# A query projection at the start of a decoder layer: turns of shift moved into the third panel, the fourth panel run unit by unit

## The chip, the cores and the metric

The kernel runs on one core of one Trainium2 chip. Five engines work beside each other, each through its own queue in order: TensorE (PE in the profile; its weight loads are PEld), VectorE (DVE), ScalarE (ACT), GpSimd (POOL) and SyncE (SP), which only issues transfers here. They meet in on-chip memory (SBUF), and TensorE's results are collected in eight banks of PSUM. The metric is the time of one execution on the device in microseconds, the median of several runs. Before the change it was 1857.52 us (three runs, 1857.36 to 1859.39).

## What is computed

One layer of a decoder trunk for 1024 prompt tokens and 8 x 8 sample tokens (1088 in all), width 1024, all in float32. The part that the change touches is the beginning: a modulated RMS norm, and the first of the columns of one input projection.

```
mod = jax.nn.silu(c) @ w_mod + b_mod
shift, scale, gate = jnp.split(mod, 3, axis=-1)
h = rmsnorm(x, norm_g) * (1 + scale[:, None]) + shift[:, None]
proj = h @ w_in
(mg, u, va, za, q, k, vb, ob, zb, ig, fg, p, zc) = jnp.split(proj, split_idx, axis=-1)
```

Behind it come three branches (a spatial gate, an mLSTM with q, k, v, and a causal pooling), their merge, an output projection, the gate and a last RMS norm. All of that is left as it is, but for one operand of the gate.

## The kernel before

**Precision and panels.** Each float32 operand of a matmul is split into a high and a low part: ACT casts the high part, DVE subtracts it from the source for the low part. A product is then three matmuls, high x high, high x low, low x high. Weights come in panels of 1024 x 256; class `Stream` loads them (SP), casts and splits them in quarters of two k each (`whi` by ACT, L132, `wlo` by DVE, L101), and with `defer` set a quarter's subtraction is put off until the next quarter's cast is issued. At most eight quarters are held. A panel times all tokens is six units: two halves f of its columns by three groups g of tokens (`GROUPS`: 364, 362, 362), each unit a PSUM bank, eight k of three matmuls.

**The start.** `start` runs operations by a hand-written string of letters, `PLAN_0 + PLAN_1`. Two query panels (q0, q1) are computed from the raw x, while the norm's factor is not known yet (L614); their rows are multiplied by the factor later, on POOL, and the share of shift is added (`finish_rows`: L705 on POOL, L709 on ACT, L710 on DVE, stores at L711). That share is shift times the panel (letter s, `shift_mm`, L678, copied by ACT at L681) and then turned to columns by four small matmuls on PE and a copy on DVE (letter t, `shift_turn`, L688 and L690). Meanwhile `h_make` (letter m) makes the eight normalised activations h[0..7], high and low (DVE L653, L658, L660, ACT L656, L657), and W prepares a quarter of the third panel's weights. The letter r (`raw_rows`) copies the raw sums of a panel out of PSUM.

**Third and fourth query panel.** `b_panel` computes q2 and q3 from h. `tick` advances generators in the list `side`, `pace / 2` steps at mid-unit and again at the end of a unit; `evac` copies a finished bank to a row on ACT (L859), and the row is stored from POOL's queue (L863). `prep_some` prepares the next panel's quarters at the end of a unit. q2 runs unit by unit, with `finish_rows` of both raw panels and then `gen_factors(0)` and `(1)` beside it. q3 runs with k outermost (`kouter`): all six banks are filled together, and the copies come at the end. Beside it run `gen_factors(2)` and `(3)` and four calls of `put_t4`.

**The factors.** The next 25 panels (`seven`, from L362) take seven products of half-size blocks in place of eight. One set of operands is made of h: `gen_factors(j)` adds high and low of h[j] and h[j+4] (L765), takes four differences (L770 to L773), and splits two of the results (L207 on ACT, L208 on DVE). The fourth difference, `t4`, is split by `put_t4(j)` into the upper tokens of h[j] itself, from the 544th on, so it must come behind every read of these tokens; the original is fetched back from memory (`b12d`) later. The seven panels use other PSUM tiles, `pairs`, over the same banks; the first is `p`. `ORDER` uses `t4` last in each panel.

**Slots.** Activations, factors, rows and many others share 34 SBUF slots of 1088 columns. A slot goes to a new tile when the last instruction that touches the old one, in program order, is done; so it is with PSUM banks. `scs`, the split silu(c), is held from the start to `gen_gate`, which uses it for the gate much later (L897).

Of the kernel before, what the change touches and what calls it, by code (L numbers as in the profile page):

```python
# [8 lines left out]
F32 = mybir.dt.float32  # L9
F32R = mybir.dt.float32r  # L10
AF = mybir.ActivationFunctionType
ALU = mybir.AluOpType
# [7 lines left out]
T = TP + TS  # L20
NH = 4
KT = 8
# [14 lines left out]
class Stream:  # L37
# [111 lines left out]
    def part(self, p, which, k, cols):  # L149

        c = p["cols"]
        o = (k % 2) * c
        return p["u"][k // 2][which][:, o + cols.start : o + cols.stop]
# [5 lines left out]
class Builder:  # L159
# [95 lines left out]
                self.st.step()  # L255


    def b_panel(self, panel, acts, evac, nk=KT, kouter=False, hook=None):

        self.st.need(panel)  # L260
        part = self.st.part
        units = [(f, g) for f in range(2) for g in range(3)]

        def mms(ps, f, g, k):
            g0, n = GROUPS[g]
            ah, al = acts[k]
            fs = slice(f * 128, f * 128 + 128)
            trip = ((0, ah), (0, al), (1, ah))
            for j, (w, a) in enumerate(trip):
                self.PE.matmul(ps[:, :n], part(panel, w, k, fs), a[:, g0 : g0 + n],  # L270
                               start=(k == 0 and j == 0), stop=(k == nk - 1 and j == 2))

        if kouter:
            pss = [self.ps() for _ in units]
            for k in range(nk):
                if hook is not None:
                    hook(k)
                for (f, g), p in zip(units, pss):
                    mms(p, f, g, k)
                self.prep_some(panel, k, nk)  # L280
            self.st.used(panel)
            for (f, g), p in zip(units, pss):
                evac(f, g, p[:, : GROUPS[g][1]])
            return
        for u, (f, g) in enumerate(units):
            p = self.ps()
            for k in range(nk):
                mms(p, f, g, k)
                if k == nk // 2 - 1:
                    self.tick(self.pace / 2)  # L290
            evac(f, g, p[:, : GROUPS[g][1]])
            self.prep_some(panel, u, len(units))
            self.tick(self.pace / 2)
        self.st.used(panel)

    def a_panel(self, panel, acts, stack, evac, cols=256, order=range(9)):
# [169 lines left out]
    def start(self):  # L466
        i, V, A, G, PE, S = self.i, self.V, self.A, self.G, self.PE, self.S
# [5 lines left out]
        def nxt(key):  # L473
            cnt[key] = cnt.get(key, 0) + 1
            return cnt[key] - 1
# [23 lines left out]
        zero = self.zero = self.const([128, 64], "zero")  # L499
# [10 lines left out]
        G.memset(self.mhalf, -0.5)  # L510
        ones = self.const([128, 1], "ones")
        G.memset(ones, 1.0)
        self.scs = self.slot([128, KT, 64], F32R, name="scs")
        V.tensor_copy(self.scs, zero.unsqueeze(1).to_broadcast([128, KT, 64]))
        sc = self.const([128, KT, 9], "sc")
        A.activation(sc, cT, AF.Tanh, scale=0.5)
        V.scalar_tensor_tensor(out=sc, in0=sc, scalar=1.0, in1=cT, op0=ALU.add, op1=ALU.mult)
        V.tensor_scalar(sc, sc, 0.5, None, ALU.mult)
        A.copy(self.scs[:, :, 0:9], sc)
        V.tensor_tensor(out=self.scs[:, :, 32:41], in0=sc, in1=self.scs[:, :, 0:9].bitcast(F32), op=ALU.subtract)  # L520

        am = self.const([128, KT, 9], "am")
        sm = self.const([128, KT, 9], "sm")
# [18 lines left out]
        def mod_mul():  # L542
            n = nxt("mm")
            p = pmod[n] = self.ps()
            w = wsp.pop(n)
            for kk in range(KT):
                for j in range(2):
                    PE.matmul(p[:64, :256], self.scs[:, kk, :], w[kk // 4][j][:, kk % 4, :],
                              start=(kk == 0 and j == 0), stop=(kk == KT - 1 and j == 1))

        def mod_copy():
# [94 lines left out]
        def h_scale(eng):  # L646
            x = xs[nxt("hs")]
            eng.tensor_tensor(out=x, in0=x, in1=rb[0], op=ALU.mult)
# [52 lines left out]
            rows.append(r)  # L701

        def finish_rows(n):
            for f in range(2):
                G.tensor_tensor(out=rows[n][f], in0=rows[n][f], in1=rb[0], op=ALU.mult)  # L705
            yield
            for f in range(2):
                r = rows[n][f]
                A.activation(r[:, :TP], r[:, :TP], AF.Identity, bias=sw[n][:, f, 0:1])  # L709
                V.tensor_tensor(out=bview(r[:, smp]), in0=bview(r[:, smp]), in1=bcol(sw[n][:, f, 1:9]), op=ALU.add)  # L710
                G.dma_start(self.qd[2 * n + f], r)  # L711
                yield
            rows[n] = None
            if n:
                self.scs2 = None
                rb.clear()

        def late_const():
            self.ident = self.cload("ident")

        ops = {
            "1": mod_load, "2": x_load, "3": self.st.load, "4": late_const,
            "w": keep_warm, "S": mod_split, "M": mod_mul, "C": mod_copy, "T": mod_turn,
            "Q": square, "A": lambda: x_scale(True), "V": lambda: x_scale(False), "H": x_high, "L": x_low,
            "W": self.st.step, "P": lambda: mms("high"), "R": lambda: mms("low"),
            "e": rms_sum, "f": rms_rows, "v": lambda: h_scale(V), "g": lambda: h_scale(G), "m": h_make,
            "z": shift_split, "s": shift_mm, "t": shift_turn, "r": raw_rows,
        }
        self.st.ahead = 1
        for what in (self.PLAN_0 + self.PLAN_1).replace(" ", ""):  # L730
# [1 line left out]
        self.st.ahead = 3  # L732
        self.st.used(w1)
        self.st.defer = True
        self.side = [finish_rows(0), finish_rows(1), self.gen_factors(0), self.gen_factors(1)]
        self.B = {n: [None] * 4 for n in range(1, 8)}
        self.t2 = {}
        self.t4 = {}
        self.pace = 2
        self.b_panel(self.pan["q", 2], self.h, self.evac_rows(2, self.qd))  # L740
        self.drain()

        def hook(k):
            for j in range(2):
                if k == j + 1:
                    self.put_t4(j)
            if k in (1, 3):
                self.side = [self.gen_factors(2 + k // 2)]
            self.tick(2)
            if k in (5, 6):  # L750
                self.put_t4(k - 3)

        self.b_panel(self.pan["q", 3], self.h, self.evac_rows(3, self.qd), kouter=True, hook=hook)
        self.drain()
        self.pace = 1

    def gen_factors(self, j):
# [89 lines left out]
            G.tensor_copy(self.hs[:, k, 64:128], hl[:, TP:T].bitcast(F32))  # L847
        self.B = None

    def evac_rows(self, n, dst, scale=None):  # L850

        st = {}

        def evac(f, g, ps):
            g0, w = GROUPS[g]
            if g == 0:
                st[f] = self.slot([128, T], name="row")
            if scale is None:
                self.A.copy(st[f][:, g0 : g0 + w], ps)  # L859
            else:  # L860
                self.A.mul(st[f][:, g0 : g0 + w], ps, scale)
            if g == 2:
                self.G.dma_start(dst[2 * n + f], st.pop(f))  # L863

        return evac

    def gen_gate(self):

        i, V, S, PE = self.i, self.V, self.S, self.PE
        row = self.slot([9, D], name="gate")  # L870
        bm = self.slot([9, D], name="bgate")
        S.dma_start(bm, i["bmodg"].partition_broadcast(9))

        def load(n):
            if n == 4:
                return None
            w = []
            for j in range(2):
                raw = self.slot([128, 4, 256], name="wg")
                S.dma_start(raw, i["w_mod"][8 + n][:, j * 4 : j * 4 + 4, :])  # L880
                w.append([raw, None, None])
            return w

        nxt = load(0)
        yield
        for n in range(4):
            w = nxt
            for j in range(2):
                w[j][1:] = [self.slot([128, 4, 256], F32R, name="wgs") for _ in range(2)]
                self.split(*w[j])  # L890
                yield
            nxt = load(n + 1)
            yield
            p = self.ps()
            for k in range(KT):
                for j in (1, 2):
                    PE.matmul(p[:64, :256], self.scs[:, k, :], w[k // 4][j][:, k % 4, :],  # L897
                              start=(k == 0 and j == 1), stop=(k == KT - 1 and j == 2))
            r = row[:, n * 256 : n * 256 + 256]
            self.A.copy(r, p[32:41, :256])  # L900
            V.tensor_tensor(out=r, in0=r, in1=p[0:9, :256], op=ALU.add)
            V.tensor_tensor(out=r, in0=r, in1=bm[:, n * 256 : n * 256 + 256], op=ALU.add)
            yield
        V.tensor_scalar(row, row, 0.5, None, ALU.mult)
        self.G.dma_start(self.gated, row)
        self.scs = None
        yield


# [936 lines left out]
for _name, _c0, _cnt in _BLOCKS:  # L1846
# [8 lines left out]
    "LPSSRPR1WS3"  # L1855
)
Builder.PLAN_1 = (
    "rW13SeSM1CPP3MS3PCfRTSgMCgPWSvRgTMgCRTvRTPzmWRmsmgPmPWmWgPRRmtms3R3WmW3tr"
)


# [103 lines left out]
```

## Time and profile before

| | |
|---|---|
| median of three runs | 1857.52 us |
| the profiled execution | 1857.86 us, of which its span 1856.1 us |
| mean granted clock of TensorE | 0.985 |
| the third panel's first matmul (L270) | 119.31 us |
| the first matmul of the seven panels (L362) | 176.87 us |

The profile is of one execution, and its times count from the span's start. A row of a timeline gives start, duration, engine, line, operation, what is written and read, the shapes and, in brackets, how long the engine stood idle before it and what ended that. "x6" means six such instructions merged, with the time of all. The list of waits sums such idle times by what ended them. The table by windows gives for each stretch the busy time of PE, PEld, DVE, ACT and POOL with the number of instructions, then TensorE's granted clock (1.00 is full), the share of the transfer engines and GB/s.

### The profile page before, as it was taken

What the parts mean: (1) busy time and instruction counts of PE and PEld (TensorE: products, weight loads), DVE (VectorE), ACT (ScalarE), POOL (GpSimd) and SP (SyncE); (2) the same over time, 40 slices, a digit from 0 to 9 for tenths busy, and PEclk for the clock granted to TensorE, in tenths of its full rate; (3) what the DMA queues carried; (4) which work ended last, traced back from release to release, by engine and by line L of the source; (5) the groups of instructions that cost most, each with busy time, mean ns of one, the idle gap of its engine ahead of it and who ended that gap; (6) DMA issues with size and microseconds to landing.
All of it is one profiled execution on the core that took longest, in us unless ns stands there. A gap on an engine that the chain in (4) does not pass through costs nothing.

```text
span 1856.1 us, 32242 instructions
## 1 busy us (share of the span) xinstructions
PE 1796.1 (97%) x13017; PEld 1777.4 (96%) x13017; DVE 1071.9 (58%) x2003; ACT 586.0 (32%) x1141; POOL 262.3 (14%) x427
## 2 busy tenths in 40 slices
PE   7888999999999999999999999999999999999998
PEld 7888999999999998999999899999999999999998
DVE  7777556665666542434527955664655766564444
ACT  5443333333333332222223125332333231131224
POOL 3440000000000001110011212321101101200023
PEclk8988999999999999999999999999999999999999
DMA  6332323332222334333335754776457577694422
GB/s 252 108 128 74 106 94 94 104 122 80 71 70 76 130 106 150 121 123 101 94 116 189 217 180 125 240 237 201 143 175 231 179 228 208 184 317 142 151 62 97
DMA packets 142152, 270.42 MB, mean 146 GB/s; under 512 B 19377, under 2 KB 66161, under 8 KB 142003
## 3 DMA queue, kind: packets, MB, share of 16 engines
q1 hardware_dynamic: 118786, 184.20, 31.4%
q0 software_dynamic: 23072, 83.91, 13.3%
q8 instruction: 102, 1.67, 0.4%
q14 instruction: 48, 0.39, 0.1%
q10 hardware_dynamic: 144, 0.26, 0.0%
HBM read 179.96 MB, written 88.35 MB: 145 GB/s over the span
## 4 chain that ended last, share of the span: by engine, by line
PE 86%; DVE 8%; issue 2%; DMA 2%; ACT 1%; POOL 1%; SPq 0%; POOLq 0%; DVEq 0%; ACTq 0%
PE ps L270 30%; PE ps L308 15%; PE p L362 8%; PE y L362 8%; PE z L362 8%; PE x L362 4%; PE ps L614 2%; PE ps L316 1%; PE ps L1466 1%; PE ps L1264 1%; PE ps L1485 1%; PE ps L1682 1%; PE ps L1439 1%; PE ps L1468 1%; DMA ss<-in_w_mod_dram 1%
## 5 line engine op out<-in xcount | busy, mean ns | idle before, releaser
L101 DVE TENSOR_TENSOR wlo<-raw,whi 128x512 fp32r<-128x512 f32 (+1 forms) x272 | 189.7, 698 | 115.6 <-ACT whi L132 115.6
L308 PE MATMUL ps<-whi,hhi 128*128 128x256 f32 (+1 forms) x768 | 218.5, 284 | 0.0
L308 PE MATMUL ps<-wlo,hhi 128*128 128x256 f32 (+1 forms) x768 | 216.0, 281 | 0.0
L308 PE MATMUL ps<-whi,hlo 128*128 128x256 f32 (+1 forms) x768 | 215.1, 280 | 0.0
L270 PE MATMUL ps<-hhi,whi 128*128 128x362 f32 (+1 forms) x624 | 208.2, 334 | 5.5 <-DVE C L1494 3.4
L270 PE MATMUL ps<-hlo,whi 128*128 128x362 f32 (+1 forms) x624 | 207.0, 332 | 1.9 <-DMA hlo<-b12d 1.7
L270 PE MATMUL ps<-hhi,wlo 128*128 128x362 f32 (+1 forms) x624 | 206.6, 331 | 0.0
L270 PE MATMUL ps<-yhi,whi 128*128 128x362 f32 (+1 forms) x576 | 190.1, 330 | 3.0 <-DVE mgr L1742 1.6
L270 PE MATMUL ps<-yhi,wlo 128*128 128x362 f32 (+1 forms) x576 | 188.7, 328 | 0.0
L270 PE MATMUL ps<-ylo,whi 128*128 128x362 f32 (+1 forms) x576 | 188.5, 327 | 0.0
L132 ACT CAST whi<-raw 128x512 fp32r<-128x512 f32 (+1 forms) x272 | 162.3, 617 | 44.9 <-DVE raw L123 36.3
L308 PEld LDWEIGHTS ps<-whi,hhi 128*128 128x128 f32 x768 | 144.6, 188 | 0.8 <-issue 0.4
L308 PEld LDWEIGHTS ps<-wlo,hhi 128*128 128x128 f32 x768 | 144.7, 188 | 0.0
L308 PEld LDWEIGHTS ps<-whi,hlo 128*128 128x128 f32 x768 | 144.4, 188 | 0.0
L270 PEld LDWEIGHTS ps<-hhi,whi 128*128 128x128 f32 x624 | 119.2, 191 | 6.7 <-DVE C L1494 3.6
L362 PE MATMUL p<-hhi,whi 128*128 128x272 f32 x400 | 116.1, 290 | 7.3 <-ACT row L859 7.3
L270 PEld LDWEIGHTS ps<-hlo,whi 128*128 128x128 f32 x624 | 119.5, 191 | 2.6 <-DMA hlo<-b12d 2.6
L270 PEld LDWEIGHTS ps<-hhi,wlo 128*128 128x128 f32 x624 | 119.4, 191 | 0.0
L362 PE MATMUL p<-hlo,whi 128*128 128x272 f32 x400 | 116.5, 291 | 0.0
L362 PE MATMUL p<-hhi,wlo 128*128 128x272 f32 x400 | 116.3, 291 | 0.0
L132 ACT CAST whi<-sum 128x512 fp32r<-128x512 f32 x75 | 46.6, 621 | 219.7 <-DVE sum L119 144.0
L270 PEld LDWEIGHTS ps<-yhi,whi 128*128 128x128 f32 x576 | 108.2, 188 | 3.7 <-DVE mgr L1742 1.8
(434 smaller groups left out, 4489.6 us busy)
## 6 DMA issues: line engine op xcount, KB each, us to landing
raw<-in_w_in_dram SPq DMA_DIRECT2D x204, 256.0 KB
mgr<-mgd SPq DMA_DIRECT2D x24, 544.0 KB
raw<-in_w_br_dram SPq DMA_DIRECT2D x48, 256.0 KB
out_dram<-C POOLq DMA_DIRECT2D x36, 256.0 KB, 4.5
ylo<-yd SPq DMA_DIRECT2D x16, 544.0 KB
merd<-mgr POOLq DMA_DIRECT2D x16, 544.0 KB, 6.1
C<-in_state_C_dram SPq DMA_DIRECT2D x32, 256.0 KB
mgd<-mg POOLq DMA_DIRECT2D x14, 544.0 KB, 4.6
```

Of the source, the lines that this page charges most:

```text
L101: self.kb.V.tensor_tensor(out=lo, in0=src, in1=hi.bitcast(F32), op=ALU.subtract)
L132: kb.A.copy(hi, src)
L270: self.PE.matmul(ps[:, :n], part(panel, w, k, fs), a[:, g0 : g0 + n], start=(k == 0 and j == 0), stop=(k == nk - 1 and j == 2))
L308: self.PE.matmul(p[:, :cols], a[:, ts], part(panel, w, k, cs), start=(k == 0 and j == 0), stop=(k == KT - 1 and j == 2))
L316: self.PE.matmul(p[:, :cols], stack[:, k, :], part(panel, j, k, cs), start=(k == 0 and j == 0), stop=(k == KT - 1 and j == 1))
L362: PE.matmul(bank[n][:, g, :HT], w[:, ks], b[:, gs], start=(n in (1, 5, 6, 7) and j == 0 and m == 0), stop=(j == 3 and m == 2), skip_group_ ...
L614: PE.matmul(sums[-1][u][:, :m], self.st.part(w, 1 - ww, k, fs), a[:, g0 : g0 + m], start=(k == 0 and part == "high" and j == 0), stop=(k = ...
L1264: self.PE.matmul(p[:, :n], wsl[:, ww, k, fs], a[:, g0 : g0 + n], start=(k == 0 and j == 0), stop=(k == 1 and j == 2))
L1439: PE.matmul(x["ps"][:, h * 128 : h * 128 + 128], k[:, 2 * h + d, :], q[:, 2 * h + d, :], start=(d == 0), stop=(d == 1))
L1466: PE.matmul(p[:, :258], x["qw"][:, 2 * h + d, :], C[x["hp"]][:, h, d, :], start=(d == 0), stop=False)
L1468: PE.matmul(p[:, :258], x["P"][:, a, h, :], x["vs"][:, b, h, :], start=(x["c"] == 0 and j == 0), stop=(j == 2))
L1485: PE.matmul(p[:, :258], x["ks"][:, a, h, d * 128 : d * 128 + 128], x["vs"][:, b, h, :], start=(j == 0), stop=(j == 2))
```

## The change

`shift_turn` leaves the plan (both letters t are gone) and becomes the first thing of `finish_rows`. All four `gen_factors` are in the side list from the third panel on, with a pace of 2.4 where it was 2; the list isn't drained between the two panels. The fourth panel runs unit by unit too, in the order 2, 1, 0, 5, 4, 3, that is, for each half of the columns the upper tokens first. After its third unit the list is drained; `put_t4` follows after the fifth unit (j = 0, 1) and after the sixth (j = 2, 3). `evac_rows` counts the parts of a row, since they come in another order. `scs` is no longer kept: `gen_gate` makes it again from `sc`.

```diff
-    def b_panel(self, panel, acts, evac, nk=KT, kouter=False, hook=None):
+    def b_panel(self, panel, acts, evac, nk=KT, kouter=False, hook=None, order=(0, 1, 2, 3, 4, 5)):
...
-        units = [(f, g) for f in range(2) for g in range(3)]
+        units = [divmod(u, 3) for u in order]
...
             evac(f, g, p[:, : GROUPS[g][1]])
             self.prep_some(panel, u, len(units))
             self.tick(self.pace / 2)
+            if hook is not None:
+                hook(u)
         self.st.used(panel)
...
         def finish_rows(n):
+            shift_turn()
             for f in range(2):
                 G.tensor_tensor(out=rows[n][f], in0=rows[n][f], in1=rb[0], op=ALU.mult)
             yield
...
-        self.side = [finish_rows(0), finish_rows(1), self.gen_factors(0), self.gen_factors(1)]
+        self.side = [finish_rows(0), finish_rows(1)] + [self.gen_factors(j) for j in range(4)]
...
-        self.pace = 2
+        self.pace = 2.4
         self.b_panel(self.pan["q", 2], self.h, self.evac_rows(2, self.qd))
-        self.drain()
-
-        def hook(k):
-            for j in range(2):
-                if k == j + 1:
-                    self.put_t4(j)
-            if k in (1, 3):
-                self.side = [self.gen_factors(2 + k // 2)]
-            self.tick(2)
-            if k in (5, 6):
-                self.put_t4(k - 3)
-
-        self.b_panel(self.pan["q", 3], self.h, self.evac_rows(3, self.qd), kouter=True, hook=hook)
-        self.drain()
+
+        def hook(u):
+            if u == 2:
+                self.drain()
+            if u > 3:
+                for j in range(2):
+                    self.put_t4(2 * u - 8 + j)
+
+        self.b_panel(self.pan["q", 3], self.h, self.evac_rows(3, self.qd), hook=hook, order=(2, 1, 0, 5, 4, 3))
...
-            if g == 0:
-                st[f] = self.slot([128, T], name="row")
-            if scale is None:
-                self.A.copy(st[f][:, g0 : g0 + w], ps)
-            else:
-                self.A.mul(st[f][:, g0 : g0 + w], ps, scale)
-            if g == 2:
-                self.G.dma_start(dst[2 * n + f], st.pop(f))
+            if f not in st:
+                st[f] = [self.slot([128, T], name="row"), 0]
+            self.A.copy(st[f][0][:, g0 : g0 + w], ps)
+            st[f][1] += 1
+            if st[f][1] == 3:
+                self.G.dma_start(dst[2 * n + f], st.pop(f)[0])
...
+        scs = self.slot([128, KT, 64], F32R, name="scs")
+        V.tensor_copy(scs, self.zero.unsqueeze(1).to_broadcast([128, KT, 64]))
+        self.A.copy(scs[:, :, 0:9], self.sc)
+        V.tensor_tensor(out=scs[:, :, 32:41], in0=self.sc, in1=scs[:, :, 0:9].bitcast(F32), op=ALU.subtract)
...
-    "rW13SeSM1CPP3MS3PCfRTSgMCgPWSvRgTMgCRTvRTPzmWRmsmgPmPWmWgPRRmtms3R3WmW3tr"
+    "rW13SeSM1CPP3MS3PCfRTSgMCgPWSvRgTMgCRTvRTPzmWRmsmgPmPWmWgPRRmms3R3WmW3r"
```

The rest of the diff renames `self.scs` to a local `scs` in `start` and keeps `sc` as `self.sc`.

More of the change, by code (lines that the diff above doesn't have):

```diff
@@ L512, in start @@
         G.memset(ones, 1.0)
-        self.scs = self.slot([128, KT, 64], F32R, name="scs")
-        V.tensor_copy(self.scs, zero.unsqueeze(1).to_broadcast([128, KT, 64]))
-        sc = self.const([128, KT, 9], "sc")
+        scs = self.slot([128, KT, 64], F32R, name="scs")
+        V.tensor_copy(scs, zero.unsqueeze(1).to_broadcast([128, KT, 64]))
+        sc = self.sc = self.const([128, KT, 9], "sc")
         A.activation(sc, cT, AF.Tanh, scale=0.5)
@@ L518, in start @@
         V.tensor_scalar(sc, sc, 0.5, None, ALU.mult)
-        A.copy(self.scs[:, :, 0:9], sc)
-        V.tensor_tensor(out=self.scs[:, :, 32:41], in0=sc, in1=self.scs[:, :, 0:9].bitcast(F32), op=ALU.subtract)
+        A.copy(scs[:, :, 0:9], sc)
+        V.tensor_tensor(out=scs[:, :, 32:41], in0=sc, in1=scs[:, :, 0:9].bitcast(F32), op=ALU.subtract)
         am = self.const([128, KT, 9], "am")
@@ L547, in mod_mul @@
                 for j in range(2):
-                    PE.matmul(p[:64, :256], self.scs[:, kk, :], w[kk // 4][j][:, kk % 4, :],
+                    PE.matmul(p[:64, :256], scs[:, kk, :], w[kk // 4][j][:, kk % 4, :],
                               start=(kk == 0 and j == 0), stop=(kk == KT - 1 and j == 1))
@@ L726, in start @@
             "e": rms_sum, "f": rms_rows, "v": lambda: h_scale(V), "g": lambda: h_scale(G), "m": h_make,
-            "z": shift_split, "s": shift_mm, "t": shift_turn, "r": raw_rows,
+            "z": shift_split, "s": shift_mm, "r": raw_rows,
         }
@@ L848, in seven_panels, with evac_rows @@
         self.B = None
-    def evac_rows(self, n, dst, scale=None):
+    def evac_rows(self, n, dst):
         st = {}
@@ L872, in gen_gate @@
         S.dma_start(bm, i["bmodg"].partition_broadcast(9))
+        scs = self.slot([128, KT, 64], F32R, name="scs")
+        V.tensor_copy(scs, self.zero.unsqueeze(1).to_broadcast([128, KT, 64]))
+        self.A.copy(scs[:, :, 0:9], self.sc)
+        V.tensor_tensor(out=scs[:, :, 32:41], in0=self.sc, in1=scs[:, :, 0:9].bitcast(F32), op=ALU.subtract)
         def load(n):
@@ L896, in gen_gate @@
                 for j in (1, 2):
-                    PE.matmul(p[:64, :256], self.scs[:, k, :], w[k // 4][j][:, k % 4, :],
+                    PE.matmul(p[:64, :256], scs[:, k, :], w[k // 4][j][:, k % 4, :],
                               start=(k == 0 and j == 1), stop=(k == KT - 1 and j == 2))
@@ L905, in gen_gate @@
         self.G.dma_start(self.gated, row)
-        self.scs = None
         yield
```

## The prediction

> **What bounds the kernel now.** I read the page's list of engines and its chain of work first, then the list of waits of TensorE, then the timelines around the two largest.
>
> ```profile
> span 1856.1 us, 32242 instructions
> PE 1796.1 (97%) x13017; PEld 1777.4 (96%) x13017; DVE 1071.9 (58%) x2003; ACT 586.0 (32%) x1141; POOL 262.3 (14%) x427
> ...
> PE ps L688 <- ACT smp L681: 8.0, 1, 8.0
> PE p L362 <- ACT row L859: 7.3, 1, 7.3
> ```
>
> TensorE (PE) is the bound: busy 97% of the span. Time can only be won where it waits or runs at a lower clock. Its two longest waits both lie in the stage that the change rewrites: 8.0 us ahead of the turns of shift (L688), 7.3 us between the fourth query panel and the first seven-panel. They are one event each, so each is worth its full length if nothing takes its place.
>
> The first wait, in the timelines of POOL, DVE, ACT and PE:
>
> ```profile
> 109.13 4.92 POOL L705 TENSOR_TENSOR row<-row,rb 128x1088 f32<-128x1088 f32 x2
> ...
> 106.17 7.97 DVE L653 TENSOR_TENSOR x<-x,sm 128x64 f32<-128x64 f32 x1
> ...
> 114.18 0.24 ACT L657 CAST hhi<-x 128x64 fp32r<-128x64 f32 x1 [10.35 <-DVE x L653]
> ...
> 117.94 0.36 ACT L681 COPY smp<-ps 64x256 f32<-64x256 f32 x1
> ...
> 106.73 0.61 PE L688 MATMUL ps<-c_sel,smp 64*128 64x9 f32 x4
> ...
> 109.18 1.15 PE L614 MATMUL ps<-xlo,whi 128*128 128x364 f32 x6
> 118.36 1.02 PE L688 MATMUL ps<-c_sel,smp 64*128 64x9 f32 x4 [8.03 <-ACT smp L681]
> ```
>
> The reader should follow it backwards. The second turn (118.36) needs a copy that ACT makes at 117.94. That copy stands in ACT's queue behind L657, which waited 10.35 us for a small add on DVE (L653). The add took 7.97 us and ended at 114.14, when POOL's multiplies ended (109.13 + 4.92 = 114.05): DVE is blocked by POOL. So **the copy is late, and with it all that ACT and DVE prepare for the third panel**. The turn is only the first instruction to meet the delay.
>
> The second wait:
>
> ```profile
> 172.93 0.62 ACT L132 CAST whi<-raw 128x512 fp32r<-128x512 f32 x1 [2.26 <-DVE raw L123]
> 173.46 1.19 ACT L207 CAST hhi<-fac 128x544 fp32r<-128x544 f32 x2
> 174.55 2.27 ACT L859 COPY row<-ps 128x364 f32<-128x364 f32 x6
> ...
> 176.87 0.60 PE L362 MATMUL p<-hhi,whi 128*128 128x272 f32 x1 [7.27 <-ACT row L859]
> ```
>
> All six banks of the fourth panel finish together, and their copies (174.55, x6) are queued on ACT behind casts that wait for DVE's factor work. PE starts again when the last copy is done (174.55 + 2.27 = 176.82).
>
> Both waits also cost clock. In the table by windows, the column after POOL is the granted clock:
>
> ```profile
> 35.00:36.00 1.00, 0.65 (x3) 0.65 (x4) 1.00 (x2) 0.00 (x0) 0.00 (x0) 0.85 0.04 16
> 42.00:43.00 1.00, 1.00 (x6) 1.00 (x5) 1.00 (x2) 1.00 (x2) 0.00 (x0) 0.74 0.03 8
> ...
> 114.00:115.00 1.00, 0.00 (x0) 0.00 (x0) 1.00 (x2) 0.82 (x3) 0.05 (x1) 0.60 0.00 0
> ...
> 124.00:125.00 1.00, 1.00 (x6) 1.00 (x6) 0.00 (x0) 0.00 (x0) 0.00 (x0) 0.78 0.01 4
> ...
> 35.35 1.91 PE L614 MATMUL ps<-xlo,whi 128*128 128x364 f32 x6 [3.80 <-DVE xlo L601]
> ```
>
> Full clock is 1.00 and the low one 0.50, so 0.60 over 114 to 115 puts the drop at 114.20, and 0.78 puts the return at 124.44. An idle of 3.80 us ended at 35.35; the drop came at 35.70 and the return at 42.52. The steps between these four times, 6.82, 71.68 and 10.24, are 2, 21 and 3 times 3.41: the clock changes on a beat.
>
> **The change part by part: first wait.** The turns leave the plan and go into the third panel: the first after half of its first unit, the second after its second unit. POOL's multiply of the rows comes after the turn in program order but uses nothing of it, so it still starts at 109.13 and still blocks DVE until 114.1. What PE can do instead is the first unit, limited by the panel's weights, four quarters of two k each, a high half cast by ACT and a low half made by DVE:
>
> ```profile
> 114.33 0.61 ACT L132 CAST whi<-raw 128x512 fp32r<-128x512 f32 x1
> 118.21 0.62 ACT L132 CAST whi<-raw 128x512 fp32r<-128x512 f32 x1
> 120.01 0.62 ACT L132 CAST whi<-raw 128x512 fp32r<-128x512 f32 x1
> ...
> 115.40 0.68 DVE L101 TENSOR_TENSOR wlo<-raw,whi 128x512 fp32r<-128x512 f32 x1
> 121.25 0.68 DVE L101 TENSOR_TENSOR wlo<-raw,whi 128x512 fp32r<-128x512 f32 x1
> ...
> 119.78 0.51 PE L270 MATMUL ps<-hlo,whi 128*128 128x364 f32 x1
> 120.08 0.51 PE L270 MATMUL ps<-hhi,wlo 128*128 128x364 f32 x1
> 125.72 0.33 PE L270 MATMUL ps<-hhi,whi 128*128 128x362 f32 x1
> 129.69 0.33 PE L270 MATMUL ps<-hhi,whi 128*128 128x362 f32 x1
> ```
>
> These are the second to fourth quarters; the first is there before. PE does two k (6 matmuls) by about 110.7, then is idle until the second quarter's cast (114.33 + 0.61 = 114.94), needs its low half at 116.08, does the rest of that quarter and the four small matmuls of the turn, and waits for the third quarter at 118.83. The turn may wait for a bank that ACT's copy empties at 118.30, so I let the second half of the unit start at 119.3. An idle of 4.3 us is longer than the one at 35.35 after which the clock fell, so I take the low clock: a matmul every 0.30 us (120.08 less 119.78). Twelve of them end at 119.3 + 3.6 = 122.9; the last low half (121.25 + 0.68 = 121.93) is in time for the ninth. Today the unit ends at 125.72. With the clock back at 124.44 as now, the second unit has done 5 matmuls by then and needs 19 more at 0.1655 (129.69 less 125.72, by 24): it ends at 127.6. The second turn adds 0.54 (106.73 to the next instruction at 107.27; the 0.61 overlaps it). So the third unit starts at 128.1 instead of 129.69: **1.5 us won, not 8**. The bounds come from the beat: with the clock back one beat earlier the same count gives 2.6, one beat later 0.0.
>
> [...]
>
> **Second wait.** The fourth panel now runs unit by unit, so five of six copies are made while later units run. Copies lag a unit's end as here:
>
> ```profile
> 125.98 0.46 ACT L859 COPY row<-ps 128x364 f32<-128x364 f32 x1 [4.26 <-PE ps L270]
> ...
> 136.21 1.28 DVE L765 TENSOR_TENSOR fac<-hhi,hlo 128x1088 f32<-128x1088 f32 x1
> 172.22 0.68 DVE L123 TENSOR_TENSOR raw<-raw,raw 128x512 f32<-128x512 f32 x1
> 174.13 0.72 DVE L208 TENSOR_TENSOR hlo<-fac,hhi 128x544 fp32r<-128x544 f32 x1 [1.23 <-ACT hhi L207]
> ...
> 169.03 1.65 ACT L207 CAST t<-fac 128x1088 fp32r<-128x1088 f32 x2 [3.83 <-DVE fac L771]
> ...
> 130.42 5.04 POOL L705 TENSOR_TENSOR row<-row,rb 128x1088 f32<-128x1088 f32 x2
> ```
>
> 0.26 after the boundary at 125.72, plus 0.46, plus 0.05 to the waiter, is 0.77: that stays of the 7.27, and 6.5 goes, if ACT is free then. Whether it is free hangs on DVE's factor chain. Today it runs from 136.21 to 172.22, 36.0 us nearly without a gap. In the new order it also holds L123 (0.7) before its end and loses two splits of upper factors (0.72 each, with one wait like the 1.23 shown): 36.0 + 0.7 - 1.4 - 1.2 = 34.1. It starts after POOL's second pair (130.42), which follows from the first unit's copy through ACT's L709 and POOL's queue; that copy comes 2.8 earlier, so the chain starts at about 133.4 and ends at 167.5. ACT's last casts for it end 1.5 before (today at 169.03 + 1.65 = 170.68 against 172.22): 166.0. Behind them ACT makes two copies (2.27 by 6 is 0.38 each) and two casts of upper factors (1.19 the two): free at 168.0. PE ends the sixth unit 1.5 earlier than today (176.87 - 7.27 = 169.6), at 168.1, and its copy wants ACT at 168.4. **The chain just fits, by 0.4 us.** The last two upper splits come behind that copy, and their factor is read last in the next panel.
>
> ```profile
> 182.47 0.42 PE L362 MATMUL y<-t,whi 128*128 128x272 f32 x2
> ...
> 242.83 0.29 PE L362 MATMUL p<-hhi,whi 128*128 128x272 f32 x1
> ...
> 245.85 0.41 PE L362 MATMUL y<-t,whi 128*128 128x272 f32 x2
> ```
>
> With 0.77 us of idle I take the clock to stay up. Its price now: the first 24 matmuls of the next panel take 5.60 us (176.87 to 182.47), later ones 3.02 (242.83 to 245.85): 2.6 won.
>
> **At nothing:** shift's operands for the gate are made again later:
>
> ```profile
> L514 DVE CAST scs<-zero x1: 427/427/427, 0.9 to 0.9; 128x512 fp32r<-128x512 f32 x1
> ```
>
> 0.43 on DVE and two operations on 72 columns instead of 512, once, ahead of PE work that waits for its own weights; without that cover under 1.3 us (three times the row). No DMA is added; the row store only fires when three parts are in, whatever their order. One slot of 34 is freed.
>
> **Sum:** 1.5 + 6.5 + 2.6 = 10.6. The profiled execution took 1857.86 us, 1.76 around its span; 1857.86 - 10.6 = 1847.3. The median shown is 0.34 lower, so I say 1847.0. Everything after 183 is PE work at full clock with few waits, so the gain should stay.
>
> **The rivals.** *The first wait is given back.* The low clock lasts one beat longer, so lead 0.0: gain 9.1, 1848.4. For it: the beat; against it: nothing else. Chance 0.17.
>
> *The factor chain is late.* [...] For it: the copies now stand between the casts in one queue. Chance 0.14.
>
> *A light window drops the clock* though PE idles only 0.77: 2.6 of the sum goes, 1849.6. Chance 0.05.
>
> *Slower: slots.* With all four factors alive (16 activations, 8 + 4 products, 4 sums) 32 of the 34 slots are held besides the rows. If factor tiles get slots whose rows are still being stored, DVE waits for each store, at most 6.0 us:
>
> ```profile
> DMA to landing us min/median/max: 3.0/4.1/6.0
> ```
>
> Three such waits make the chain 18 late, 17.6 after slack: the clock falls again, and 10.6 - 2.6 - 17.6 = -9.6 gives about 1867. It decides from 8.4 us late. Against it: the stores before were long landed. Chance 0.04.
>
> *The change doesn't do what it says:* a wait of PE remains at the panel's end as long as now; only the 1.5 stays, 1855.5. Chance 0.03.
>
> **How the numbers follow.** The forecast has 0.57, its own range 1845.0 to 1849.0 (lead 2.6 to 0.0, copies one microsecond late). With the first rival and the mild half of the second and third, 1844.5 to 1852.0 leaves less than 2 in 10 out. A measurement tells about 0.2% (3.7 us) from no change. Faster by more: all but the slot case, the last rival and the worst of the chain, 0.90; within: 0.06; slower: 0.04.
>
> **What would show it.** L688 no longer among PE's waits; an idle of about 4 us after 110, ended by casts of L132; the panel ending near 168; the wait at L362 under 1 us and the clock 1.00 there; DVE's last factor split near 167.5. A wait at L362 of several us, ended by L859 behind L207, would mean the chain is late; a DMA ending DVE's idle there would mean slots.

## The result, and the profile after

| | before | changed | ratio (95% interval) |
|---|---|---|---|
| first comparison, medians | 1857.47 us (4 runs) | 1847.35 us (4 runs, 1843.83 to 1848.12) | 0.9944 (0.9930 to 0.9957) |
| second comparison, medians | 1858.36 us (15 runs) | 1848.70 us (5 runs, 1845.20 to 1849.63) | 0.9956 (0.9943 to 0.9968) |
| the profiled execution | 1857.86 us, span 1856.1 | 1843.83 us, span 1842.1 | |

The change makes the kernel about 10 us faster, 0.5%. Its profiled execution is the fastest of the first four: it lies 14 us under the profiled one of before, 4 us more than the medians do. The last section comes back to these 4 us.

The list of TensorE's waits in the changed kernel (engine, line and tile, what ended the wait, us in total, times, longest):

```profile
PE ps L270 <- ACT whi L132: 4.4, 1, 4.4
...
PE p L364 <- ACT row L856: 1.3, 1, 1.3
...
PE ps L690 <- ACT smp L683: 0.6, 1, 0.6
```

The wait of 8.0 us at the turns (now L690) is 0.6, and a new wait of 4.4 us stands in its place, ended by a cast of the third panel's weights. The wait ahead of the seven panels (now L364) fell from 7.3 to 1.3. The timelines of DVE, POOL, ACT and PE around the first:

```profile
104.42 8.00 DVE L655 TENSOR_TENSOR x<-x,sm 128x64 f32<-128x64 f32 x1
...
104.89 2.55 POOL L650 TENSOR_TENSOR x<-x,rb 128x1088 f32<-128x1088 f32 x1
107.38 4.94 POOL L708 TENSOR_TENSOR row<-row,rb 128x1088 f32<-128x1088 f32 x2
...
112.60 0.61 ACT L132 CAST whi<-raw 128x512 fp32r<-128x512 f32 x1
...
113.27 0.67 PE L270 MATMUL ps<-hhi,whi 128*128 128x364 f32 x1 [4.36 <-ACT whi L132]
121.45 0.33 PE L270 MATMUL ps<-hhi,whi 128*128 128x362 f32 x1
```

The small add is still blocked for 8.00 us, beside three multiplies of POOL, until POOL is done (107.38 + 4.94 = 112.32); the cast still follows it, and TensorE, which has done two k of its first unit, waits for that cast. The second unit starts at 121.45.

The table by windows (as before: busy times, then the granted clock) shows the low clock in this unit and the full one ahead of the seven panels:

```profile
112.40:121.40 9.00, 7.41 (x22) 6.07 (x23) 8.92 (x19) 7.03 (x14) 0.00 (x0) 0.51 0.22 61
121.40:128.00 6.60, 6.60 (x42) 6.35 (x41) 1.88 (x7) 4.57 (x7) 3.01 (x3) 1.00 0.62 205
165.40:168.00 2.60, 1.33 (x9) 1.03 (x8) 2.60 (x5) 2.60 (x7) 0.46 (x1) 1.00 0.00 0
```

And the end of the fourth panel, in the timelines of DVE, ACT and PE:

```profile
156.42 1.93 DVE L208 TENSOR_TENSOR t<-fac,t 128x1088 fp32r<-128x1088 f32 x2 [1.69 <-ACT t L207]
164.78 1.92 DVE L208 TENSOR_TENSOR t<-fac,t 128x1088 fp32r<-128x1088 f32 x2
...
154.76 0.62 ACT L132 CAST whi<-sum 128x512 fp32r<-128x512 f32 x1 [4.14 <-DVE sum L121]
155.29 1.64 ACT L207 CAST t<-fac 128x1088 fp32r<-128x1088 f32 x2
...
164.98 0.81 ACT L856 COPY row<-ps 128x362 f32<-128x362 f32 x2
165.68 1.20 ACT L207 CAST hhi<-fac 128x544 fp32r<-128x544 f32 x2
166.78 0.47 ACT L856 COPY row<-ps 128x364 f32<-128x364 f32 x1
...
167.30 0.39 PE L364 MATMUL p<-hhi,whi 128*128 128x272 f32 x1 [1.26 <-ACT row L856]
170.43 0.41 PE L364 MATMUL y<-t,whi 128*128 128x272 f32 x2
```

ACT goes without a pause from the factor's casts to two copies, two casts of upper factors and the last copy, which ends at 167.25; TensorE starts then, at full clock: its first 24 matmuls take 3.13 us (167.30 to 170.43), where they took 5.60.

**A common ruler.** Before the stage begins, executions already differ by some us. So stages are compared from the start of the blocked small add (106.17 before, 104.42 after). From the timelines of all profiles, in us after that start:

| profile | the add takes | second unit of the third panel starts | last matmul of the fourth panel starts | wait ahead of the seven panels | their first matmul | first 24 take | stage (last two added) |
|---|---|---|---|---|---|---|---|
| before | 7.97 | 19.55 | 63.10 | 7.27 | 70.70 | 5.60 | 76.30 |
| change, first profile | 8.00 | 17.03 | 61.29 | 1.26 | 62.88 | 3.13 | 66.01 |
| change, second profile | 7.99 | 17.12 | 62.37 | 0.55 | 63.25 | 3.13 | 66.38 |
| new panel only | 7.97 | 19.29 | 62.83 | 1.97 | 65.13 | 4.64 | 69.77 |
| turns only | 7.98 | 17.12 | 61.65 | 7.28 | 69.25 | 4.46 | 73.71 |
| POOL's rows held back | 3.10 | 12.24 | 57.87 | 1.37 | 59.57 | 3.11 | 62.68 |
| plain order | 7.99 | 17.13 | 62.06 | 0.55 | 62.93 | 3.13 | 66.06 |
| wait filled | 8.03 | 17.18 | 62.41 | 0.55 | 63.30 | 3.12 | 66.42 |
| scs kept | 7.99 | 17.04 | 61.30 | 2.50 | 64.13 | 4.64 | 68.77 |
| held back, plain, pace 2.5 | 3.10 | 12.24 | 56.94 | 1.47 | 58.73 | 3.13 | 61.86 |
| the same, pace 2.64 | 3.11 | 13.33 | 59.76 | 0.55 | 60.63 | 3.13 | 63.76 |

The stage of the change is 10.3 and 9.9 us shorter than that of before.

### The profile page after: what moved, and what is told of

Read it like the earlier page. It is cut to its first block, busy times and chain, and to the rows that moved or that the text cites. A ratio compares the mean times of both kernels' runs of the same rounds, so it can differ in the third digit from the quotient of the medians.

```text
span 1842.1 us, 32227 instructions
## 1 busy us (share of the span) xinstructions
PE 1792.3 (97%) x13017; PEld 1773.2 (96%) x13017; DVE 1074.0 (58%) x2005; ACT 585.4 (32%) x1142; POOL 260.6 (14%) x427
## 3 DMA queue, kind: packets, MB, share of 16 engines
q8 instruction: 102, 1.67, 0.4%
## 4 chain that ended last, share of the span: by engine, by line
PE 86%; DVE 7%; issue 3%; ACT 2%; DMA 1%; POOL 1%; SPq 0%; POOLq 0%; DVEq 0%; ACTq 0%
PE ps L270 31%; PE ps L310 15%; PE y L364 8%; PE p L364 8%; PE z L364 8%; PE x L364 4%; PE ps L616 2%; PE ps L318 1%; PE ps L1465 1%; PE ps L1263 1%; PE ps L1484 1%; PE ps L1438 1%; PE ps L1681 1%; PE ps L1467 1%; PE ps L550 1%
## 5 line engine op out<-in xcount | busy, mean ns | idle before, releaser
L364 PE MATMUL p<-hhi,whi 128*128 128x272 f32 x400 | 115.0, 287 | 1.3 <-ACT row L856 1.3
L364 PE MATMUL p<-hlo,whi 128*128 128x272 f32 x400 | 115.3, 288 | 0.0
L364 PE MATMUL p<-hhi,wlo 128*128 128x272 f32 x400 | 115.2, 288 | 0.0
```

The lines of the kernel that those rows point to most:

```text
L364: PE.matmul(bank[n][:, g, :HT], w[:, ks], b[:, gs], start=(n in (1, 5, 6, 7) and j == 0 and m == 0), stop=(j == 3 and m == 2), skip_group_ ...
```

## The experiments

**The change once more**, without an edit.

> The changed kernel once more, beside the other three of this group, so that all four have the same runs of the kernel before. Theory: 10.1 us faster than before (1847.4), with a spread of some 3 us between executions that comes from where the beat of the clock falls after the first wait. Rival, that the first profile of it (1843.8) is the rule and the others are disturbed: 13 to 14 us faster.

Measured: 1848.70 us against 1858.36, 9.7 faster; five executions from 1845.20 to 1849.63. The first profile's 1843.83 was the quickest execution, not the rule.

**The new panel only.**

```diff
         def finish_rows(n):
-            shift_turn()
...
-    "...PRRmms3R3WmW3r"
+    "...PRRmtms3R3WmW3tr"
```

> The turns of shift are back in the plan, all the rest of the change is kept. Theory (the first wait gives only about 1.5 us, because the panel's weights and activations are late anyway): 8 to 9.5 us faster than before, 1 to 2 us slower than the change, and the wait of 8 us at the turns is back. Rival (moving the turns is worth the 4 us by which the wait became shorter, and the clock with it): 5 us faster than before, 5 us slower than the change.

Measured: 1848.13 us, ratio 0.9959 (0.9947 to 0.9971), so 5.4 to 9.8 us faster than before. By time it can't be told from the change. The wait of 8.0 us at the turns is back. In the stage it loses 3.4 to 3.8 us to the change, more than expected, and the ruler says where: the last matmul comes 0.5 to 1.5 later, the wait ahead of the seven panels is 1.97 long, and behind it the low clock returns for one beat (173.4 to 176.8, worked out from the windows), so that the first 24 matmuls take 4.64. The windows of this kernel there:

```profile
172.00:174.00 2.00, 0.94 (x5) 0.95 (x6) 2.00 (x4) 2.00 (x5) 0.53 (x1) 0.85 0.00 0
174.00:176.00 2.00, 2.00 (x11) 2.00 (x10) 1.60 (x3) 0.09 (x1) 0.00 (x0) 0.50 0.89 240
176.00:178.00 2.00, 2.00 (x15) 2.00 (x14) 0.00 (x0) 0.04 (x1) 0.00 (x0) 0.79 0.41 170
```

TensorE is idle from 171 to 173 only, and has half the clock at 174. This execution was also the slowest of its five (1851.67), so the profile shows the bad case. Neither expectation held in full: most of the gain comes from the fourth panel, as the theory says; how much the turns add within the change is between nothing and 3.8 us, and by medians (1848.13 against 1848.70) it is nothing.

**The turns only.** The kernel before, with `shift_turn()` at the head of `finish_rows` and both letters t gone from the plan.

> Only the turns are moved into the third panel, the fourth panel stays with k outermost. Theory: 1 to 2 us faster than before; the wait of about 4.4 us ended by the cast of the panel's second quarter stays, and the second wait of 7.3 us stays. Rival (the parts need each other: without the new fourth panel the lead is lost again in the factor chain of DVE, since the second wait ends with it): 0 to 0.5 us faster.

Measured: 1854.05 us (11 runs), ratio 0.9982 (0.9973 to 0.9991): 1.7 to 5.0 us faster. The waits are as the theory has them:

```profile
PE p L362 <- ACT row L860: 7.3, 1, 7.3
PE ps L270 <- ACT whi L132: 4.3, 1, 4.3
PE ps L688 <- ACT smp L681: 0.6, 1, 0.6
```

The lead at the end of the fourth panel is 63.10 - 61.65 = 1.45 us, and it isn't lost: the seven panels start 1.45 earlier. That decides against the rival. Between medians the gain is 4.3, more than the 1 to 2 expected. In the stage it is 2.6: the lead, and 1.1 less for the first 24 matmuls, because the low clock behind the second wait lasted two beats here (172.8 to 179.7) and three before (172.2 to 182.5). Whether the edit has a part in that isn't shown, and the rest of the 4.3 stays open. The two halves of the change alone, 10.2 and 4.3 between medians, add up to more than the 9.7 of the whole, so the times don't split the gain; the stage has to.

**POOL's rows held back.** The wait behind the first wait, tested by moving POOL's work instead of the waiter:

```diff
         def finish_rows(n):
             shift_turn()
+            if n == 0:
+                late = self.const([128, 1], "late")
+                G.tensor_copy(late, self.pan["q", 2]["u"][3][1][:, 0:1].bitcast(F32))
             for f in range(2):
                 G.tensor_tensor(out=rows[n][f], in0=rows[n][f], in1=rb[0], op=ALU.mult)
```

> The change, with POOL's first multiply of raw rows held back until DVE has made the last low quarter of the third panel's weights (POOL first copies one column of that quarter). Theory (POOL's multiplies block DVE's small add for 8 us, and that is what is behind the wait of 4.4 us): the add takes under 3.5 us, the wait of TensorE at the second quarter shrinks from 4.4 to under 1.5 us, the first unit ends 4 to 5.5 us earlier; but the factor chain can't come as much earlier, so the wait ahead of the seven panels grows by about 2 us: 2 to 5 us faster than the change, 12 to 15 faster than before. Rival (the add waits for its own input, not for POOL): the add still ends where it did, and the kernel is as fast as the change or slower by what POOL's rows come later.

Measured: 1844.98 us, ratio 0.9942 (0.9927 to 0.9956), 8.2 to 13.6 us faster than before. By time it can't be told from the change, whose interval overlaps; in the stage it is 3.3 and 3.7 faster than the change's two profiles. DVE's and POOL's timelines, and the list of TensorE's waits:

```profile
104.94 3.10 DVE L655 TENSOR_TENSOR x<-x,sm 128x64 f32<-128x64 f32 x1
118.43 3.06 DVE L101 TENSOR_TENSOR wlo<-raw,whi 128x512 fp32r<-128x512 f32 x1 [1.27 <-ACT whi L132]
...
105.41 2.54 POOL L650 TENSOR_TENSOR x<-x,rb 128x1088 f32<-128x1088 f32 x1
115.82 0.18 POOL L709 COPY late<-wlo 128x1 f32<-128x1 f32 x1 [7.87 <-DVE wlo L101]
115.96 4.99 POOL L711 TENSOR_TENSOR row<-row,rb 128x1088 f32<-128x1088 f32 x2
...
PE p L364 <- ACT row L859: 1.4, 1, 1.4
PE ps L690 <- ACT smp L683: 1.2, 1, 1.2
```

The add falls from 8 to 3.10 us and now ends with the one multiply of POOL that is left there (105.41 + 2.54 = 107.95); the moved multiplies block another DVE operation at their new place (118.43, 3.06 instead of 0.68). The block is shown: it follows POOL's work. It isn't one instruction that waits for one other: in the change the add outlasts two multiplies that POOL starts at 107.38 or later, 3 us after the add. The add took 8.00 us beside three multiplies, 3.10 beside one; by what means POOL holds DVE up isn't shown here.

The wait at the panel's second quarter is gone, and the first unit ends 4.8 us earlier than in the change (12.24 after 17.03). The seven panels start only 3.3 and 3.7 earlier. DVE's factor chain sets that, as expected: it starts at 129.09 where it was 131.89, which is 3.3 earlier after the add's start, and the last copy stands behind its casts. TensorE itself comes 3.4 and 4.5 earlier to the end of the fourth panel; against the first profile it had already lost 1.4 in the second unit, in a low clock that lasted until 15.3 after the add's start. So the wait grew by 0.1 and 0.8, less than the 2 us named.

**Plain order of units**, all splits of upper factors at the end:

```diff
         def hook(u):
             if u == 2:
                 self.drain()
-            if u > 3:
-                for j in range(2):
-                    self.put_t4(2 * u - 8 + j)
+            if u == 5:
+                for j in range(4):
+                    self.put_t4(j)
 
-        self.b_panel(self.pan["q", 3], self.h, self.evac_rows(3, self.qd), hook=hook, order=(2, 1, 0, 5, 4, 3))
+        self.b_panel(self.pan["q", 3], self.h, self.evac_rows(3, self.qd), hook=hook)
```

> The change with the fourth panel in its plain order of units (0 to 5), and all four splits of upper factors after the sixth unit. Theory (what counts is that copies are made unit by unit; the upper tokens first buy nothing, since the split factor is read some 18 us into the next panel, and two of its casts stand ahead of the last copy in ACT's queue): the wait ahead of the seven panels is 0 to 1.2 us shorter than in the change, the time within 1.5 us of it, 9 to 12 us faster than before. Rival (the order is what makes room: four splits in a row after the panel hold up ACT and DVE for the seven panels): a new wait of TensorE of 2 us or more within the first seven-panel, 2 to 4 us slower than the change.

Measured: 1845.86 us, ratio 0.9934 (0.9920 to 0.9948), 9.7 to 14.9 faster than before. The stage, 66.06, is the change's own; no new wait of 2 us. ACT's last copy waits 0.91 us for TensorE, where in the change it stood behind two casts. Upper tokens first bring nothing that these times or the stage show.

**The wait filled.** TensorE works in the wait of 4.4 us; the forty products are never read.

```diff
                 mms(p, f, g, k)
+                if warm and u == 0 and k == 1:
+                    for _ in range(warm):
+                        self.PE.matmul(p[:, 368:512], part(panel, 0, 0, slice(0, 128)), acts[0][0][:, 0:144],
+                                       start=True, stop=True, skip_group_check=True)
```

> The change, and in the wait of 4.4 us TensorE does 40 matmuls of 144 columns into unused columns of the first unit's bank; their results are never read. Theory (the wait costs its length and then the low clock, which lasts whole beats of 3.41 us at 1.7 us each): the granted clock stays 1.00 from 107 to 122, the first unit ends about 1 us earlier, limited by the panel's last quarter, and the second is at full speed at once: 1 to 2.5 us faster than the change, 10.5 to 13 faster than before. Rival (the low clock lies under other waits and costs nothing more): as fast as the change, or slower by what the filling runs over (under 1 us).

Measured: 1850.48 us, ratio 0.9962 (0.9950 to 0.9975), 4.6 to 9.3 faster than before. The theory failed here. By time the run can't be told from the change, whose intervals overlap. PE's timeline:

```profile
108.77 4.59 PE L291 MATMUL ps<-hhi,whi 128*128 128x144 f32 x40
116.54 0.75 PE L694 MATMUL ps<-c_sel,smp 64*128 64x9 f32 x4 [1.21 <-ACT smp L687]
```

and the table by windows, two of one beat each:

```profile
113.43:116.84 3.41, 1.67 (x9) 1.06 (x9) 3.41 (x8) 2.99 (x6) 0.00 (x0) 1.00 0.21 77
116.84:120.25 3.41, 3.35 (x12) 2.65 (x11) 3.33 (x8) 3.06 (x7) 0.00 (x0) 0.50 0.27 77
```

The filling held the clock through the wait, and then it fell all the same, at 116.84, after a beat in which TensorE was busy for 1.67 of 3.41 us and never idle longer than 1.21. The second unit started at 17.18, as without it. The stage, 66.42, is that of the change's second profile (66.38).

**The slot of scs kept.** `scs` stays in `self` and `gen_gate` uses it, as before the change.

```diff
-        scs = self.slot([128, KT, 64], F32R, name="scs")
+        scs = self.scs = self.slot([128, KT, 64], F32R, name="scs")
...
-        scs = self.slot([128, KT, 64], F32R, name="scs")
-        V.tensor_copy(scs, self.zero.unsqueeze(1).to_broadcast([128, KT, 64]))
-        self.A.copy(scs[:, :, 0:9], self.sc)
-        V.tensor_tensor(out=scs[:, :, 32:41], in0=self.sc, in1=scs[:, :, 0:9].bitcast(F32), op=ALU.subtract)
+        scs = self.scs
```

> The change with the split silu(c) kept in its slot from the start to the gate, as before, so that one slot less is free. Theory (slots are not what holds the factor chain): within 1 us of the change apart from the beat of the clock, and no idle time of DVE or ACT in the two panels that a transfer ends. Rival (the freed slot is what lets all four factors be alive at once): DVE or ACT waits 3 to 6 us for a store of a query row, and the wait ahead of the seven panels grows to 3 us or more, 3 to 6 us slower than the change.

Measured: 1847.49 us (4 runs), ratio 0.9951 (0.9938 to 0.9965), the change's time. No transfer ends a wait of DVE or ACT in the two panels, but a slot does, in ACT's list of waits between 160 and 170 and in the timelines of DVE and ACT:

```profile
ACT whi L132 <- DVE raw L123: 4.7, 1, 4.7
ACT row L856 <- DVE t L208: 1.1, 1, 1.1
...
165.54 1.92 DVE L208 TENSOR_TENSOR t<-fac,t 128x1088 fp32r<-128x1088 f32 x2
166.91 0.82 ACT L856 COPY row<-ps 128x362 f32<-128x362 f32 x2 [1.08 <-DVE t L208]
```

The copy of the fourth unit needs a new row, and its slot is that of the last factor, which DVE is still reading. That 1.1 us puts the wait ahead of the seven panels at 2.50, and a beat of low clock followed it (4.64 for the first 24 matmuls). So the freed slot is worth 1.1 us at that copy; with the beat the stage of this profile is 2.4 and 2.8 longer than the change's two. The time can't resolve it.

**All of it, with a pace of 2.5:** POOL's rows held back, plain order, `self.pace = 2.5`.

> POOL's first rows held back as in the run before, the plain order of units with all splits of upper factors after the sixth, and a pace of 2.5, so that the third factor's split comes ahead of the stream's sum, which cost DVE an idle of 1.69 us. Theory (after POOL's block is gone the factor chain of DVE and ACT's queue set the end of the panel; each of the three edits shortens it): the wait ahead of the seven panels under 0.8 us, the seven panels start 3.5 to 5 us earlier after POOL's block than in the change: 13 to 16 us faster than before. Rival (what is left ahead of the seven panels is the plain delay of the last copy, and the pace changes nothing): as fast as the run that only holds the rows back, 12 to 13.5 us.

Measured: 1842.95 us, ratio 0.9925 (0.9913 to 0.9938), 11.5 to 16.2 faster than before; the stage is 4.1 to 4.5 shorter than the change's. The wait ahead of the seven panels was 1.47, not under 0.8. DVE's and ACT's timelines:

```profile
161.66 1.93 DVE L208 TENSOR_TENSOR t<-fac,t 128x1088 fp32r<-128x1088 f32 x2 [1.69 <-ACT t L207]
...
160.01 0.62 ACT L132 CAST whi<-raw 128x512 fp32r<-128x512 f32 x1 [5.54 <-DVE raw L123]
160.53 1.64 ACT L207 CAST t<-fac 128x1088 fp32r<-128x1088 f32 x2
```

The gap of 1.69 us only moved, from the third factor to the last: its casts stood behind the cast of the stream's third sum in ACT's queue. On this point the rival is right: what the pace was changed for brought nothing. The interval of the time holds both expectations; the stage is 0.8 shorter than with the rows held back alone.

**The same with a pace of 2.64**, and the owed steps begun at -0.4, so that both the turn and the last factor change places with what they waited for.

```diff
-        self.pace = 2.5
+        self.pace = 2.64
+        self.owed = -0.4
```

> The fastest version so far (POOL's rows held back, plain order), with a pace of 2.64 and the count of owed steps begun at -0.4. The first turn of shift then stands behind the third panel's first unit instead of in its middle, where it waited 1.21 us for ACT, and the last factor's casts are issued ahead of the stream's third sum, behind which they cost DVE 1.69 us. Theory (in the end ACT's order of casts and copies sets the wait ahead of the seven panels): that wait falls from 1.47 to under 0.8 us, the wait at the turn is gone, the stage from POOL's block to the second seven-panel is 1 to 2 us shorter; the time 13.5 to 16 us faster than before, which one run of five rounds can't tell from the version without these edits. Rival (DVE's total work bounds the panel, whatever its order): the wait ahead of the seven panels stays at 1.3 us or more, and DVE works without a gap up to the last factor.

Measured: 1841.69 us (4 runs, 1837.91 to 1843.39), ratio 0.9906 (0.9890 to 0.9923), 14.3 to 20.4 faster than before. The list of waits:

```profile
PE ps L270 <- ACT whi L132: 1.7, 1, 1.7
PE p L364 <- ACT row L860: 0.5, 1, 0.5
```

Both edits did what they were for: no wait at the turn, 0.5 ahead of the seven panels, and DVE without a gap up to the last factor. The stage of its profile is 1.9 longer than the one before it, against the expectation: TensorE met a wait of 1.7 us at a weight cast in the third panel, and by the windows the low clock behind the first unit lasted three beats (10.2 us) where it lasted one (3.4) in the run before. The profiles are also opposite extremes, the slowest of these executions and the quickest of those. It and the run before are the fastest versions, and which of the two is faster isn't settled.

## Why the prediction was right

**The first wait: 1.5 us, not 8.** Right in its steps: POOL's multiply was not moved by the edit and blocked the add for 8.00 us; the new wait is 4.36 for 4.3; the clock fell in it, at 111.1 (0.53 over 111 to 112). The first unit ends 17.0 after the start of the add where the working gives 122.9 - 106.17 = 16.7. Holding POOL back shows the cause that was only read from the page. The lead at the end of the fourth panel lies inside the bounds of 0.0 and 2.6, but that it comes out near the middle is luck. In the five profiles with this wait of 4.3 to 4.4 us and nothing put into it, the low clock lasted three beats (10.24 us) each time, and the later it ended the less of the lead was left (ends worked out from windows of one microsecond, as in the prediction):

| profile | low clock ends, us after the add's start | lead, us |
|---|---|---|
| change, first profile | 16.9 | 1.81 |
| scs kept | 16.9 | 1.80 |
| turns only | 17.7 | 1.45 |
| plain order | 18.6 | 1.04 |
| change, second profile | 19.3 | 0.73 |

The prediction put the end at 124.44 - 106.17 = 18.3, where it happened to be in the one profile before.

**The second wait: 0.77 left of 7.27.** Right in kind; 1.26 and 0.55 are left. "The chain just fits, by 0.4 us" did not hold in the first profile: it ends at 164.78 + 1.92 = 166.70, that is 62.3 after the add's start, where the working has 167.5 - 106.17 = 61.3. What the working lacked is DVE's gap of 1.69 us ahead of 156.42: the third factor's casts stand in ACT's queue behind the cast of the stream's second sum. Counting in exact numbers, the step is due at the middle of the unit, ahead of that sum: fifteen times 1.2 is 18. In the program's own addition, fifteen times 1.2 leaves 0.9999999999999991 of a step owed after 17 steps, short of the 1 that is needed, and step 18 slips to the end of the unit. Whether ACT is free in time then depends on the lead: in the first profile (lead 1.8) the copy came 0.5 late, in the second (lead 0.7) it came on time. So part of a longer lead is given back here: the leads differ by 1.1, the starts of the seven panels only by 0.4.

**The clock: 2.6 us.** 5.60 less 3.13 is 2.47. The price is itself a matter of the beat: in the turns alone, with two beats of low clock where there were three, the same 24 matmuls took 4.46.

**Nothing for the gate.** The three operations ran at 1079.2 to 1081.8 us with 0.42, 0.26 and 0.24 us, far ahead of their use. The freed slot, entered at nothing, is worth 1.1 us at one copy.

**The sum.** 10.6 forecast; 10.3 and 9.9 in the stage, 10.1 and 9.7 between medians. By terms the stage has 1.8 + 6.0 + 2.5 and 0.7 + 6.7 + 2.5: a long lead and a late copy offset each other.

**The rivals.** *The first wait is given back* is one end of the spread found, 0.7 of lead in the second profile; but the low clock did not last a beat longer there, it came later. *The factor chain is late* came by 0.5 us in one profile and not in the other. *A light window drops the clock* did not happen in the two profiles of the change (1.26 and 0.55 us of wait), but it did with 1.97 us (the new panel alone) and 2.50 us (scs kept), where the first 24 matmuls took 4.64. No run shows a length of idle from which the clock falls: ahead of the seven panels half speed followed these two waits and not those of 0.55 to 1.47 us. *Slots* as priced, behind stores, did not appear; a slot held by DVE did, at 1.1 us, once one slot less was there.

## What to carry to other kernels

An instruction that waits is often only the first to meet a delay: before moving it, ask what is queued behind the thing that it waits for. Here moving the waiter won 0.7 to 1.8 of 8 us, and moving POOL's multiply, which nothing in the list of TensorE's waits names, another 3.3 to 3.7 of the stage. In ACT's queue the order of casts and copies was a resource of its own: copying results unit by unit won 6.0 to 6.7 us by letting five of six copies go ahead of that queue's late part, and a step that slips by a rounded fraction cost 1.7 us on DVE.

## What was not expected of the hardware

**The spread of executions goes with the clock.** Time and mean granted clock of the nine executions of the change:

```
1843.83  0.989      1848.70  0.985
1847.06  0.986      1845.20  0.988
1848.12  0.985      1849.29  0.985
1847.64  0.985      1847.55  0.986
                    1849.63  0.985
```

Over 1845 us one thousandth of the mean is 3.7 us at half speed, so at most 1.85 us of work, and less where TensorE waits in them. From 0.985 to 0.989 that is at most 7.4; the quickest execution is 3.8 to 5.8 us ahead of the five at 0.985. By windows of one microsecond its profile has 41 us of low clock, the second profile 56. Where its length is given above, the low clock lasted 3.4, 6.9 or 10.2 us, one to three beats of 3.41, and the beat falls differently on the work in each profile, as the table of leads shows. That is why differences of 2 us in single runs tell nothing here, and why the stage was compared on a ruler of its own; the ruler takes out what comes before the stage, not the beat within it.

**A long idle is not needed for the low clock.** Beats in which TensorE was busy 1.67 of 3.41 us and never idle longer than 1.21 (the filled wait), or idle for 1.97 us between full work (the new panel alone), were followed by half speed. The waits of 0.55 to 1.47 us ahead of the seven panels were not. The busy time of the profile alone doesn't mark the border: in the run with a pace of 2.5, half speed followed a beat with 2.20 of 3.41 us busy (110.87 to 114.28, four matmuls of 9 columns among it), but not one with 2.16 (162.06 to 165.47). What does mark it is not shown here.
